# A streaming GLU kernel: stores moved to GpSimd's software queue, merged tile instructions, and fewer waits

## Chip, cores, metric

The kernel runs on one core of a Trainium2 chip. The metric is device time in microseconds (us) of one execution, median of several; all runs used below for a verdict are in the fast state (for one core: not over 1.5% above the fastest run of the same kernel). Profiles are of one execution each, and their span is some 2 us shorter than the device time.

## The reference

```python
# x: 8192 x 8192 float32, out: 8192 x 4096 float32
a, b = np.split(x, 2, axis=-1)
return a * (1 / (1 + np.exp(-b)))
```

So 268.44 MB come in, 134.22 MB go out, and each output element takes one sigmoid and one product.

## The kernel before

32 tiles; a tile is 128 partitions of two consecutive rows each, so one partition holds 64 KB of input and 32 KB of output, both contiguous in memory. There are two slots of each buffer. Loads are issued by SyncE, stores by ScalarE, both through hardware queues.

```python
R = 2
n_tiles = n_rows // (P * R)
x_t = x.rearrange("(n p r) m -> n p (r m)", p=P, r=R)
out_t = out.rearrange("(n p r) m -> n p (r m)", p=P, r=R)
pool = ctx.enter_context(tc.tile_pool(name="io", bufs=2))
for i in range(n_tiles):
    x_sb = pool.tile([P, R * n_cols], fp32)
    o_sb = pool.tile([P, R * half], fp32)
    load = nc.sync.dma_start(out=x_sb, in_=x_t[i])
    n = 4 if i == n_tiles - 1 else 1        # the last tile in 8 pieces
    w = half // n
    for r in range(R):
        for c in range(n):
            # ... a, b, cols: the piece's two inputs and its output columns
            nc.scalar.activation(out=b, in_=b, func=SIG)
            nc.vector.tensor_mul(out=o_sb[:, cols], in0=a, in1=b)
            if n > 1:
                nc.scalar.dma_start(out=out_t[i, :, cols], in_=o_sb[:, cols])
    if n == 1:
        nc.scalar.dma_start(out=out_t[i], in_=o_sb)
# ... the first load is moved ahead of the start barrier
```

## Time and profile before

| | before |
|---|---|
| device time, median of 6 runs | 936.02 us (935.64 to 936.99) |
| span of the profiled run | 933.9 us |
| DMA | 402.67 MB, 431 GB/s over the span |
| VectorE, ScalarE busy | 30%, 25% |
| load / store, issue to landing | 45.5 / 41.7 us |
| one tile every | 29.0 us |

Read it from the DMA rows down. The engines that compute are idle for 70 and 75% of the span, the DMA engines never; the two landing times are longer than the 29.0 us in which a tile passes, so in both queues a transfer stands behind its predecessor. The prediction shows and reads the lines.

### The profile page before, as it was taken

Reading aid. Unit: us, or ns where it says so; the run is one execution under the profiler, and the core shown is the slowest. Engines: PE = TensorE matmul, PEld = TensorE weight load, DVE = VectorE, ACT = ScalarE, POOL = GpSimd, SP = SyncE. Lnnn points to the kernel's source line nnn. Section 1 sums busy time; section 2 is a strip of 40 time slices with the busy share of each in tenths; the row PEclk is TensorE's granted clock in tenths of the full one; section 3 lists DMA queues with packets and bytes.
Section 4 is the critical chain, followed back from the end, with each engine's and each line's share of the span. In section 5 each row is a group of like instructions: output and inputs, shape, how many; then the busy total and the mean of one; then the engine's idle time right before and its main releaser. Section 6 shows DMA issues by size and latency. Waiting matters only on the chain.

```text
span 933.9 us, 410 instructions
## 1 busy us (share of the span) xinstructions
DVE 280.9 (30%) x70; ACT 230.0 (25%) x71; POOL 0.2 (0%) x4
## 2 busy tenths in 40 slices
DVE  0333321333213333133331333312333123331234
ACT  1313331133311333203332033320233202333023
POOL 0000000000000000000000000000000000000000
DMA  9999999999999999999999999999999999999998
GB/s 404 420 434 431 453 418 429 439 434 449 420 456 404 452 424 427 449 425 451 412 459 410 438 438 425 451 421 452 413 449 421 431 445 443 429 420 453 410 446 362
DMA packets 10226, 402.67 MB, mean 431 GB/s; under 512 B 1136, under 2 KB 1136, under 8 KB 2160
## 3 DMA queue, kind: packets, MB, share of 16 engines
q1 hardware_dynamic: 4608, 268.44, 66.5%
q10 hardware_dynamic: 5616, 134.22, 33.3%
q14 instruction: 2, 0.02, 0.0%
HBM read 268.44 MB, written 134.22 MB: 431 GB/s over the span
## 4 chain that ended last, share of the span: by engine, by line
DMA 78%; DVE 15%; ACT 6%; issue 0%; DVEq 0%; ACTq 0%
DMA x_sb<-in_x_dram 78%; DVE o_sb L39 15%; ACT x_sb L38 6%; DVEq L61 0%; ACTq L41 0%; ACTq L38 0%
## 5 line engine op out<-in xcount | busy, mean ns | idle before, releaser
L39 DVE TENSOR_TENSOR o_sb<-x_sb 128x4096 f32<-128x4096 f32 (+1 forms) x70 | 280.9, 4056 | 647.2 <-ACT x_sb L38 647.2
L38 ACT ACTIVATE x_sb<-x_sb 128x4096 f32<-128x4096 f32 (+1 forms) x70 | 228.7, 3315 | 695.9 <-DMA x_sb<-in_x_dram 691.8
L38 ACT ACT_TABLE_LOAD x1 | 1.3, 1283 | 0.8 <-PEq L85 0.8
L85 POOL MEMSET const-uint8-127<- 128x1 uint8 x1 | 0.1, 103 | 0.0
L85 POOL MEMSET const-bfloat16-1.0<- 128x1 bf16 x1 | 0.1, 102 | 0.0
L85 POOL MEMSET const-float32-0.0<- 128x1 f32 x1 | 0.1, 99 | 0.2 <-issue 0.2
L85 POOL MEMSET const-float32-1.0<- 128x1 f32 x1 | 0.1, 99 | 0.0
## 6 DMA issues: line engine op xcount, KB each, us to landing
out_dram<-o_sb ACTq DMA_DIRECT2D x31, 4096.0 KB, 41.7
out_dram<-o_sb ACTq DMA_DIRECT2D x8, 512.0 KB, 6.2
x_sb<-in_x_dram SPq DMA_DIRECT2D x32, 45.5
```

The lines of the kernel that those rows point to most:

```text
L38: nc.scalar.activation(out=b, in_=b, func=SIG)
L39: nc.vector.tensor_mul(out=o_sb[:, cols], in0=a, in1=b)
L85: nc = _bacc.Bacc("TRN2", target_bir_lowering=False, num_devices=1)
```

## The change

The intent: let GpSimd, which has nothing to do, issue the stores; compute each tile in one sigmoid and one product instead of two and two; and declare away every wait that follows from one that is kept, so that fewer instructions wait. In odd tiles the wait for the output slot moves from the product to the sigmoid ahead of it.

```diff
-            nc.scalar.activation(out=b, in_=b, func=SIG)
-            nc.vector.tensor_mul(out=o_sb[:, cols], in0=a, in1=b)
...
-    if n == 1:
-        nc.scalar.dma_start(out=out_t[i], in_=o_sb)
+    load = nc.sync.dma_start(out=xs[i % SLOTS], in_=x_t[i])
+    implied(load, *old["loads"], *old["sigs"])
...   # parts: tile 0 in two halves, tiles 1 to 30 whole, the last in eight pieces
+    for k, (r, c) in enumerate(parts):
+        b = rows[:, r, 1, c]
+        sig = nc.scalar.activation(out=b, in_=b, func=SIG)
+        mul = nc.vector.tensor_mul(out=packed[:, r, c], in0=rows[:, r, 0, c], in1=b)
+        implied(sig, *old["sigs"], *old["muls"], *old["loads"])
+        implied(mul, *old["muls"], *old["loads"], *now["loads"])
+        by_sigmoid = i % 2 == 1 and len(parts) == 1
+        implied(mul, *(s for s in old["stores"] if by_sigmoid or s not in freed))
+        if by_sigmoid:
+            for s in freed:
+                tc.add_manual_dep(sig.ins, s.ins.name, DEP, reason="frees the output slot")
...
+    now["stores"].append(nc.gpsimd.dma_start(out=out_t[i], in_=os[i % SLOTS]))
```

More of the change, by code (lines that the diff above doesn't have):

```diff
@@ L11, in _tiles @@
     P = nc.NUM_PARTITIONS
+    DEP = mybir.DependencyInfo(mybir.DependencyClass.Sync, mybir.DependencyReason.DATA)
     fp32 = mybir.dt.float32
@@ L17, in _tiles @@
     R = 2
+    SLOTS = 2
     n_tiles = n_rows // (P * R)
@@ L20, in _tiles @@
     out_t = out.rearrange("(n p r) m -> n p (r m)", p=P, r=R)
-    pool = ctx.enter_context(tc.tile_pool(name="io", bufs=2))
-    first = None
-    for i in range(n_tiles):
-        x_sb = pool.tile([P, R * n_cols], fp32)
-        o_sb = pool.tile([P, R * half], fp32)
-        load = nc.sync.dma_start(out=x_sb, in_=x_t[i])
-        first = first or load
-        n = 4 if i == n_tiles - 1 else 1
-        w = half // n
-        for r in range(R):
-            for c in range(n):
-                lo = r * n_cols + c * w
-                a = x_sb[:, lo : lo + w]
-                b = x_sb[:, lo + half : lo + half + w]
-                cols = slice(r * half + c * w, r * half + (c + 1) * w)
-                nc.scalar.activation(out=b, in_=b, func=SIG)
-                nc.vector.tensor_mul(out=o_sb[:, cols], in0=a, in1=b)
-                if n > 1:
-                    nc.scalar.dma_start(out=out_t[i, :, cols], in_=o_sb[:, cols])
-        if n == 1:
-            nc.scalar.dma_start(out=out_t[i], in_=o_sb)
@@ L44, in _tiles, with implied @@
-    return first
+    pool = ctx.enter_context(tc.tile_pool(name="io", bufs=1))
+    xs = [pool.tile([P, R * n_cols], fp32, name=f"x_sb{k}") for k in range(SLOTS)]
+    os = [pool.tile([P, R * half], fp32, name=f"o_sb{k}") for k in range(SLOTS)]
+    def implied(later, *earlier):
+        for e in earlier:
+            tc.declare_no_dep(later.ins, e.ins, reason="follows from the waits that are kept")
+    gone = [{k: [] for k in ("loads", "sigs", "muls", "stores")} for _ in range(SLOTS)]
+    last_stores = [[] for _ in range(SLOTS)]
@@ new lines, in _tiles @@
+    for i in range(n_tiles):
+        old = gone[i % SLOTS]
+        freed = last_stores[i % SLOTS]
+        now = {k: [] for k in old}
+        rows = xs[i % SLOTS].rearrange("p (r h m) -> p r h m", r=R, h=2)
+        packed = os[i % SLOTS].rearrange("p (r m) -> p r m", r=R)
+        load = nc.sync.dma_start(out=xs[i % SLOTS], in_=x_t[i])
+        implied(load, *old["loads"], *old["sigs"])
+        now["loads"].append(load)
+        if i == 0:
+            parts = [(slice(r, r + 1), slice(0, half)) for r in range(R)]
+        elif i < n_tiles - 1:
+            parts = [(slice(0, R), slice(0, half))]
+        else:
+            w = half // 4
+            parts = [
+                (slice(r, r + 1), slice(c * w, (c + 1) * w)) for r in range(R) for c in range(4)
+            ]
+        for k, (r, c) in enumerate(parts):
[9 more added lines that the diff above has]
+                    tc.add_manual_dep(sig.ins, s.ins.name, DEP, reason="frees the output slot")
+            now["sigs"].append(sig)
+            now["muls"].append(mul)
+            if i == n_tiles - 1:
+                cols = slice(r.start * half + c.start, r.start * half + c.stop)
+                store = nc.gpsimd.dma_start(out=out_t[i, :, cols], in_=os[i % SLOTS][:, cols])
+                now["stores"].append(store)
+        if i < n_tiles - 1:
+            now["stores"].append(nc.gpsimd.dma_start(out=out_t[i], in_=os[i % SLOTS]))
+        for s in now["stores"]:
+            implied(s, *old["loads"], *old["sigs"], *old["muls"], *now["loads"], *now["sigs"])
+        for k in old:
+            old[k] += now[k]
+        last_stores[i % SLOTS] = now["stores"]
```

## The prediction

> **What bounds the kernel now.** I read the share of the 16 DMA engines first, then the DMA queues, then stretches of the span, and only then the chain of work that ended last, because the chain alone misleads here. The page says that the DMA engines are the only thing that is full:
>
> ```profile
> DVE 280.9 (30%) x70; ACT 230.0 (25%) x71; POOL 0.2 (0%) x4
> ...
> DMA  9999999999999999999999999999999999999998
> ...
> q1 hardware_dynamic: 4608, 268.44, 66.5%
> q10 hardware_dynamic: 5616, 134.22, 33.3%
> ...
> HBM read 268.44 MB, written 134.22 MB: 431 GB/s over the span
> ```
>
> Queue q1 is the loads, q10 the stores. Their packets took 66.5% + 33.3% = 99.8% of what 16 engines have in 933.9 us, that is 932 us. So the time of the packets is the whole span. Cost per byte is the same in both directions: 0.665 x 933.9 / 268.44 = 2.31 us per MB for loads and 0.333 x 933.9 / 134.22 = 2.32 us per MB for stores. Next, stretches of the span: one tile in the middle, the loading of the last tile, and the end.
>
> ```profile
> 420.00:449.00 29.00, 8.76 (x2) 7.12 (x2) 0.00 (x0) 1.00 1.00 434
> ...
> 898.25:914.69 16.44, 0.00 (x0) 0.00 (x0) 0.00 (x0) 1.00 1.00 435
> ...
> 930.00:931.00 1.00, 0.00 (x0) 0.00 (x0) 0.00 (x0) 1.00 1.00 410
> 931.00:932.00 1.00, 0.00 (x0) 0.00 (x0) 0.00 (x0) 1.00 0.43 172
> 932.00:933.00 1.00, 0.00 (x0) 0.00 (x0) 0.00 (x0) 1.00 0.04 16
> ```
>
> The last two columns are the DMA share and GB/s. A tile is 8.39 MB in and 4.19 MB out, 12.58 MB, and the tiles are 29.0 us apart: 12.58 / 29.0 = 434 GB/s at a share of 1.00. The engines stay full until about 931.4; only the first 1 to 2 us (the first packets are booked between 1 and 2 us) and the last 2.5 us are without data. The loss that any scheduling change could recover is therefore some 4 us of 934, and most of it is the latency of the first and the last transfer.
>
> Now the chain:
>
> ```profile
> 172.24 45.44 DMA x_sb<-in_x_dram
> 217.76 3.62 ACT x_sb L38
> 221.41 8.77 DVE o_sb L39 x2
> 230.20 45.41 DMA x_sb<-in_x_dram
> ```
>
> It reads as load, sigmoid, two products, next load into the same slot, every 58.0 us for two tiles. The trap is to think that compute of 12.4 us is on this path. The load issued at 172.24 does not run 45 us: another tile's data landed at 188.91 (the sigmoids there start at that time), so for its first 16.7 us it stands in its queue behind the other load, and then it moves in 28.8 us. The chain thus has 16.7 us of slack that the profile paints as DMA. The stores have such a queue too: landing is 41.7 us after issue, with one issued every 29 us, so each stands some 12.6 us behind the one before.
>
> **What the Trainium skill says.** "DMA: Bandwidth & Descriptors", section "Where 436 GB/s comes from": the fabric caps the 16 engines at 435.2 GB/s. The trace agrees: 434 to 435 in full stretches. Same page, "Queues, rings and completion order": an engine goes round its queues packet by packet. The trace agrees: a load has one row of 64 KB in each of 128 partitions and a store one of 32 KB, so packets taken in turn split the bytes 2:1. That is also what the kernel needs, and both queues indeed stay backlogged. "SWDGE vs HWDGE vs iDMA", still the same page: the software path prefers packets of at most 4096 bytes; no run shows it yet. "SBUF — State Buffer", section "Who interferes with whom": GpSimd, which writes the descriptors of its stores, shares a port pair with VectorE, but a product of two SBUF inputs collides only with GpSimd reads. No run yet shows GpSimd stores.
>
> **The change part by part.** (1) One sigmoid and one product for both rows of a tile, in 30 of 32 tiles. From the groups by shape:
>
> ```profile
> L39 DVE TENSOR_TENSOR o_sb<-x_sb 128x4096 f32<-128x4096 f32 x62 | 271.6, 4422 | 626.6 <-ACT x_sb L38 626.6
> L38 ACT ACTIVATE x_sb<-x_sb 128x4096 f32<-128x4096 f32 x62 | 220.8, 3608 | 670.1 <-DMA x_sb<-in_x_dram 670.1
> L39 DVE TENSOR_TENSOR o_sb<-x_sb 128x1024 f32<-128x1024 f32 x8 | 9.4, 1221 | 20.6 <-ACT x_sb L38 20.6
> L38 ACT ACTIVATE x_sb<-x_sb 128x1024 f32<-128x1024 f32 x8 | 7.9, 1046 | 25.9 <-DMA x_sb<-in_x_dram 21.8 <-DVE o_sb L39 4.1
> ```
>
> Two sizes give a line: sigmoid (3608 - 1046) / 3072 = 0.834 ns per element and 192 ns fixed, so 8192 elements take 7.02 us; product 1.042 ns and 154 ns, so 8.69 us. Saved: 30 x 0.19 = 5.8 us of ScalarE and 30 x 0.15 = 4.6 us of VectorE, both three quarters idle: worth 0. Lost: the product no longer starts after half the sigmoid. From landing to the end of the product it was 12.4 us; it becomes 7.02 + 8.69 + two hops of 0.03 = 15.8 us. So the next load and the store are issued 3.3 us later. The load has 16.7 us of slack: 13.4 left. The store has about 12.6: 9 left. On the path to the end: 0. The first tile keeps its halves and the last its eight pieces.
>
> (2) Waits. Odd tiles wait for the old store before the sigmoid instead of before the product. A store is issued 12.47 us after its tile landed and is through 41.7 us later, at +54.2; the tile two later lands at +58.1. The sigmoid therefore finds it done with 3.9 us to spare. If it came later by some us, it would eat from the 13.4 us of the load. The trace before has 153 semaphore instructions that stand alone (17 to 21 ns each), in engines that wait anyway; dropping some of them is worth 0.
>
> (3) Stores by GpSimd. Software has to write the descriptors first, which no row here times; with 9 us of backlog in front, some microseconds of it are worth 0 for 31 stores. Bytes are the same, so the packet time stays at 932 us if the packets stay one row each. ScalarE no longer issues stores in the last tile: it sat 4.1 us there for products, so pieces come out about a microsecond earlier. But store 30 lands 24.8 us after 898.25, at 923.05, while the last load lands at 914.69; the eight pieces need 8 x 0.52 MB / 0.434 = 9.7 us behind it, to 932.7 with receipt, and the last landed at about 933.1. So the end is full of DMA too, and earlier pieces only queue. Worth 0 to -0.5. For the software path's completion and the drain of one more engine's queue I add an estimate of 0.5 to 1 us, without a row behind it.
>
> Sum: 936.13 + 0 + 0 - 0.3 + 0.8 = about 936.6.
>
> **The rivals.** A: the software queue cuts a row of 32 KB into small packets. The end of the trace prices it: with 4 KB rows a full engine moves 410 GB/s, not 434, so 134.22 MB would take 327 instead of 309 us, +18 us. Worse, in a turn by packets loads would get nearly everything, stores would fall behind, products wait for output slots, and the load queue run dry while one store plus 15.8 us of computing pass: 1 to 5 us for each pair of tiles, +16 to +80. For it: the packet size that the skill names for that path. Against: a contiguous row needs no cut, and the hardware path cuts none (q1's 4608 packets are 4096 rows and 32 x 16 completions). Result 954 to 1030; chance 6%.
>
> B: the opposite, several rows sent per turn. Stores finish early, loads still always have work, but the last load lands later and less is left for the stores behind it; the last pieces come at landing + 12 us instead of lying in a backlog. At most 3 us: 937 to 940. Chance 10%.
>
> C: the chain as painted is real, and 3.3 us more per tile and slot lengthens it: 16 x 3.3 = +53 us, 989. Against: a DMA share of 1.00 in every inner tile; a chain that set the pace would leave gaps. 1%.
>
> D: the new path is faster by something, for instance in fewer waits. Against: the packets alone need 932 us of the 933.9. To gain 2%, the rate would have to reach 442 GB/s, above anything in a long stretch. Under 1%.
>
> **Range and chances.** The floor is stiff: below 935 nothing can come but a shorter tail, so the low end is 935.0. Upward, B and a slower completion reach 940, and part of A lies beyond; high end 941. The 2% line is 954.9, which only A and C pass: slower 0.07, faster 0.01, same 0.92.
>
> **What would show it.** Right: DMA share 9 in every slice; a software queue of 134.22 MB at about 33.3% with a packet for each row; loads landing 29.0 us apart; load time to landing shrinking from 45.5 to about 42.2, as the slack is eaten; merged sigmoid 7.0 and product 8.7 us; idle of ScalarE still ended by loads, not by stores. Wrong: many more packets in the store queue or a higher share per MB (A); sigmoids or products ended by stores, with slices of DMA under 9 (A, C); landings of stores well under 40 us with a thin tail (B).

## The result, and the profile after

| | before | after |
|---|---|---|
| device time, median of 6 runs | 936.02 us | 936.49 us (936.21 to 937.22) |
| span of the profiled run | 933.9 us | 934.7 us |
| instructions in the profile | 410 | 286 |
| semaphore instructions that stand alone, in the loop | 153 | 77 |
| load / store, issue to landing | 45.5 / 41.7 us | 42.1 / 38.2 us |

The ratio is 1.0005, 95% interval 0.9992 to 1.0018: the same. (A ratio here is the mean time of one kernel's runs over that of the other's in the same rounds, so not quite the ratio of the medians.) The page of the changed kernel, the same parts as in the prediction:

```profile
DVE 278.7 (30%) x40; ACT 227.0 (24%) x41; POOL 21.1 (2%) x43
...
DMA  9999999999999999999999999999999999999998
...
q1 hardware_dynamic: 4608, 268.44, 66.5%
q0 software_dynamic: 5616, 134.22, 33.3%
```

The stores are now in a software queue, q0. Its count of packets, its bytes and its share are those of the hardware queue before, to the digit: 5616, 134.22 MB, 33.3%. The DMA engines do the same work in the same time, and they are still full. The changed kernel's chain in order of time, and its merged instructions by shape:

```profile
117.57 42.24 DMA x_sb<-in_x_dram
159.90 7.04 ACT x_sb L66
166.96 8.70 DVE o_sb L67
175.68 42.02 DMA x_sb<-in_x_dram
```

```profile
L67 DVE TENSOR_TENSOR o_sb<-x_sb 128x8192 f32<-128x8192 f32 x30 | 260.7, 8692 | 605.7 <-ACT x_sb L66 605.7
L66 ACT ACTIVATE x_sb<-x_sb 128x8192 f32<-128x8192 f32 x30 | 210.9, 7029 | 652.2 <-DMA x_sb<-in_x_dram 652.2
```

Computing takes 3.3 us longer in each link of the chain (7.04 + 8.70 instead of 3.62 + 8.77), and the painted load is 3.4 us shorter (42.0 to 42.2 instead of 45.4), so a link still takes 58.1 us (58.0 before). The later issue was paid out of queueing. The idle time of ScalarE is still ended by loads, never by a store: the wait that moved to the sigmoid costs nothing here.

Only the end differs. The instructions that close the program, for the kernel before (columns: count, duration in ns as minimum/median/maximum, first and last start in us):

```profile
L61 POOLq DRAIN  x3: 34/41/70, 0.7 to 933.7; - x3
L61 SPq DRAIN  x3: 7/7/7, 933.2 to 933.5; - x3
```

and for the changed kernel:

```profile
L104 POOLq DRAIN  x3: 45/101/9608, 924.3 to 934.4; - x3
L104 SPq DRAIN  x3: 7/7/7, 932.7 to 934.2; - x3
```

SyncE reaches its first drain when all stores have landed: at 933.2 before, at 932.7 after. From there to the end of the span it was 0.7 us; now it is 2.0 us, because GpSimd has a drain of 9.6 us, begun after its last issue at 924.3, that holds the closing barrier until about 933.9. So -0.5 us for landing, +1.3 us for closing: +0.8 us of span, of which +0.5 us shows in the medians.

### The profile page after: what moved, and what is told of

The parts are those of the page before. It is cut to its first block, busy times and chain, and to the rows that moved or that the text cites. A ratio compares the mean times of both kernels' runs of the same rounds, so it can differ in the third digit from the quotient of the medians.

```text
span 934.7 us, 286 instructions
## 1 busy us (share of the span) xinstructions
DVE 278.7 (30%) x40; ACT 227.0 (24%) x41; POOL 21.1 (2%) x43
## 3 DMA queue, kind: packets, MB, share of 16 engines
q0 software_dynamic: 5616, 134.22, 33.3%
HBM read 268.44 MB, written 134.22 MB: 431 GB/s over the span
## 4 chain that ended last, share of the span: by engine, by line
DMA 72%; DVE 14%; ACT 11%; issue 1%; POOL 0%; POOLq 0%; ACTq 0%
DMA x_sb<-in_x_dram 72%; DVE o_sb L67 14%; ACT x_sb L66 11%; POOL out_dram L79 0%; POOLq L104 0%; ACTq L66 0%; POOLq L79 0%
## 5 line engine op out<-in xcount | busy, mean ns | idle before, releaser
L67 DVE TENSOR_TENSOR o_sb<-x_sb 128x8192 f32<-128x8192 f32 (+2 forms) x40 | 278.7, 6983 | 645.4 <-ACT x_sb L66 645.4
L66 ACT ACTIVATE x_sb<-x_sb 128x8192 f32<-128x8192 f32 (+2 forms) x40 | 225.7, 5661 | 693.7 <-DMA x_sb<-in_x_dram 693.7
L82 POOL DMA_DIRECT2D out_dram<-o_sb x31 | 16.6, 536 | 884.5 <-DVE o_sb L67 884.5
L79 POOL DMA_DIRECT2D out_dram<-o_sb x8 | 4.2, 531 | 19.1 <-DVE o_sb L67 19.1
## 6 DMA issues: line engine op xcount, KB each, us to landing
out_dram<-o_sb POOLq DMA_DIRECT2D x31, 4096.0 KB, 38.2
x_sb<-in_x_dram SPq DMA_DIRECT2D x32, 42.1
```

The lines of the kernel that those rows point to most:

```text
L66: sig = nc.scalar.activation(out=b, in_=b, func=SIG)
L67: mul = nc.vector.tensor_mul(out=packed[:, r, c], in0=rows[:, r, 0, c], in1=b)
L79: store = nc.gpsimd.dma_start(out=out_t[i, :, cols], in_=os[i % SLOTS][:, cols])
L82: now["stores"].append(nc.gpsimd.dma_start(out=out_t[i], in_=os[i % SLOTS]))
```

## The experiments

Twelve runs, each three rounds beside the kernel before. The first two take the change apart; e3, e4, e10 and e11 measure the slack; e5, e6, e9 and e12 ask what the packets and the place of a wait would do; e7 and e8 look at the end. A run can count as the same (under 2%) and still differ clear of noise, when the interval of its ratio leaves out 1.

### Stores alone: e1_stores_only

```diff
-nc.scalar.dma_start(...)        # in the kernel before, both stores
+nc.gpsimd.dma_start(...)
```

> The kernel before with nothing changed but the issuer of the stores (GpSimd instead of ScalarE). My theory (the DMA engines' packet time is the bound, and the software queue adds only something at the very end): 936.0 to 937.0 us, a span of about 934.7 us as in the changed kernel, one software queue of 134.22 MB at 33.3%, 5616 packets, share of DMA 1.00 in the middle; GpSimd's last drain ends over 1 us after the last landing. Rival (the software queue costs something in every tile, which the merged instructions give back): a tile period above 29.05 us and more than 940 us. Rival (the software queue costs nothing, the end comes from the merge): 933.9 us of span.

Measured: 937.56 us (937.28 to 938.12), ratio 1.0017 (1.0002 to 1.0032), span 935.4 us. The software queue again has 5616 packets and 33.3%; SyncE's first drain is at 933.4, the end 2.0 us later, with a GpSimd drain of 9.5 us. The closing cost is the same as in the changed kernel; the median lies 0.6 us above the range that I wrote. Nothing is lost per tile: loads land 45.5 us after issue, as before.

### Merged instructions and fewer waits alone: e2_merge_only

```diff
-nc.gpsimd.dma_start(...)        # in the changed kernel, both stores
+nc.scalar.dma_start(...)
```

> The changed kernel with its stores issued by ScalarE again, so merged instructions and fewer waits alone. The instruction order shows a side effect: in every fourth tile the store stands behind the next tile's sigmoid in ScalarE's queue, so it is issued some 20 us later. My theory: loads fill the DMA engines meanwhile and the load has 13 us of slack, so 935.5 to 936.5 us and a span of 933.5 to 934.2 us, without GpSimd's long drain at the end. Rival (merging costs time, and the software stores hide it): more than 940 us, with slices of DMA under 9.

Measured: 942.73 us (939.46 to 945.34), ratio 1.0069 (1.0045 to 1.0094). My expectation failed by 6 us; the rival's time fits, but not its gaps in the DMA row. Who waited for whom in this run:

```profile
ACT x_sb L66 <- DMA out_dram<-o_sb: 362.8, 12, 34.5
ACT x_sb L66 <- DMA x_sb<-in_x_dram: 334.7, 20, 22.1
DVE o_sb L67 <- DMA out_dram<-o_sb: 168.0, 12, 18.0
```

Sigmoids and products now wait for stores, which they do in neither kernel. In every fourth tile the store stands behind the next tile's sigmoid in ScalarE's queue, goes out late, and through the output slots the lateness reaches the loads. Slices of DMA all stay at 9, yet the load queue's share is 66.7% of 941.6 us, or 628 us for the bytes that took 621 us before: the loss is in longer load packets. So the parts of the change are not independent: with stores in ScalarE's in-order queue the merged form with its moved waits costs 0.7%, and moving the stores to GpSimd takes that away. Whether the merge or the wait that moved to the sigmoid is needed for the loss, no run separates: none has the merged form with stores by ScalarE and the wait before the product.

### More compute: e3_two_products, e4_three_products

```diff
 mul = nc.vector.tensor_mul(out=packed[:, r, c], in0=rows[:, r, 0, c], in1=b)
+if len(parts) == 1:
+    for _ in range(1):               # e4: range(2)
+        mul = nc.vector.tensor_mul(out=packed[:, r, c], in0=rows[:, r, 0, c], in1=b)
```

> The changed kernel, each merged product done twice (the same result): 8.7 us more between a load's landing and the next load into that slot, from 15.9 to 24.6 us. My theory: the load has about 13 us of slack behind the other load, so 936 to 937 us, DMA share 9 throughout, and the loads' time from issue to landing falls from 42.1 to about 33.4 us. Rival (the painted chain is real): one slot's cycle of two tiles is 8.7 us longer, 15 times 8.7 = 130 us, so about 1067 us.

Measured: 977.45 us (974.09 to 981.74), ratio 1.0445 (1.0414 to 1.0475). My expectation failed, and so did the rival's 1067. I had looked at the load's 13 us of slack and forgotten the store's 9 us, which the prediction itself gives: 8.7 us more uses it up but for some 0.5 us. In 14 tiles a sigmoid waited for a store. But the page shows something else that I had not thought of:

```profile
DMA  9999999999999999999999999999999999999997
...
q1 hardware_dynamic: 4608, 268.44, 67.3%
q0 software_dynamic: 5616, 134.22, 31.8%
```

The DMA engines are as busy as ever, and the loads' packets take 67.3% of 980.0 us, 660 us instead of 621. 39 of the 46 us more of span are in slower load packets, not in gaps. A full DMA row proves that the engines have work, not that the work goes at full rate; the cost per MB (2.46 instead of 2.31 us) is the thing to compare.

> The changed kernel, each merged product done three times: 33.3 us between landing and the next load, more than the 29.0 us in which the other slot's load lands. My theory: now the slack is used up; the load queue runs dry for about 4 us in each tile, the loads' time to landing is that of a load that starts at once (28 to 31 us), one slot's cycle of two tiles is 33.3 + 28 to 31 us, so 31 to 32 us per tile: 990 to 1030 us, and the DMA share falls below 0.95. Rival (compute never matters while VectorE is under 100%): 936 us. Rival (painted chain): two times 130, about 1197 us.

Measured: two runs at 1056 us, two at 1087 us; the profile has 1054.4 us. The direction is as expected and the size is above my range. VectorE is busy 76%, loads land 31.2 us after issue, and the DMA share in the middle is 0.90 to 0.91. In 14 tiles a sigmoid waited for a store, 397 us in all, which no run takes out here. The packet records show a second loss beside the emptied queue: a load gives each of the 16 engines eight rows, so it goes in eight rounds of packets, and the first two rounds took 3.0 and 3.1 us on average, the others 2.42 to 2.45. So the load packets take 662 us instead of 621, 40 of the 120 us more of span. The two slow rounds seem to go with different queues. The first follows an empty load queue, like the first round of the whole program, which takes 3.1 us in the kernels before and after. The second mostly ends just as the packets of a store begin after an empty store queue. Before and after have one such round too, where no load is late: the last of the second load, 3.6 us, ends at 42 us, and the first store's packets begin at 41.3 and 41.5 us.

### Half of that: e11_half_product_more

```diff
+if len(parts) == 1:
+    now["muls"].append(mul)
+    mul = nc.vector.tensor_mul(out=packed[:, 1, c], in0=rows[:, 1, 0, c], in1=rows[:, 1, 1, c])
```

> The changed kernel with only half of each merged product done a second time: 4.4 us more instead of 8.7. The change itself spent 3.3 of the store's 12.6 and the load's 16.7 us. Theory (slack is what counts, the store's 9 us being the smaller): 4.4 us fit, 936 to 937.5 us, loads landing about 37.7 us after issue, stores about 33.8. Rival (every delay costs in proportion, as 8.7 us cost 41 us): about 957 us.

Measured: 936.59 us (936.42 to 937.33), ratio 1.0006 (0.9991 to 1.0021); loads land after 37.7 us, stores after 33.7 us, both as written. 133 us more of VectorE's time cost nothing at all. So the slack is real, between 4.4 and 8.7 us of it are left in the changed kernel, and beyond it time is lost out of proportion. The issues of this run (the last number is the median time to landing):

```profile
out_dram<-o_sb POOLq DMA_DIRECT2D x31, 4096.0 KB, 33.7
...
x_sb<-in_x_dram SPq DMA_DIRECT2D x32, 37.7
```

### Is it the wait before the sigmoid? e10_two_products_late_wait

```diff
-by_sigmoid = i % 2 == 1 and len(parts) == 1     # in e3
+by_sigmoid = False
```

> The run with two products per tile again (977 us), all tiles waiting for the old store before the product. Theory W: the store, issued 8.7 us later, used up the 9 us of its backlog, and the odd sigmoid that waited for it (14 times, 336 us) made loads late; with the wait 7 us later the load is in time and the kernel is back at 936 to 942 us. Theory L (a load issued only 4 us ahead of its queue's end is what slows it, whoever is to blame): 965 to 980 us.

Measured: 979.4 us (969.08 to 980.68), ratio 1.047 (1.0453 to 1.0488). Theory W fell: now no sigmoid and no product waits for a store, and it is as slow. Two tiles early and two stretches in the middle of this run (the last two columns are DMA share and GB/s):

```profile
72.00:101.00 29.00, 17.39 (x2) 6.97 (x2) 0.53 (x1) 1.00 1.00 434
101.00:130.00 29.00, 17.39 (x2) 7.04 (x2) 0.53 (x1) 1.00 1.00 434
...
400.00:430.00 30.00, 17.38 (x2) 6.81 (x2) 0.53 (x1) 1.00 1.00 419
430.00:460.00 30.00, 17.39 (x2) 6.55 (x2) 0.53 (x1) 1.00 1.01 415
```

It starts at the full 434 GB/s with each load issued some 4.3 us ahead of its turn, and then slides to 415 at the same share. In the packet records the first two rounds of a load take 2.8 and 2.7 us on average, nearly as long as where the queue is quite empty (e4), and after the slide the starts of one round are spread over 3 to 4 us instead of 0.6 to 1.0 in the kernels before and after.

Theory L's range fits, but that a load issued too shortly before its queue runs out is what costs is not shown. The same run speaks against it as a rule: its loads were issued some 4.3 us ahead from load 3 on, and the first rounds of loads 3 to 11 (counted from 0) still took 2.42 us. A rival is untested: the stores were issued 8.7 us later too, which leaves the store queue only some 0.5 us (38.2 - 8.7 - 29.0), and e4's second slow round goes with the store queue, not with the load queue. No run makes only the loads or only the stores late. So 8.7 us of delay in both queues is too much; which queue it is, why such packets are slower, and what starts the slide stay open.

### Small packets in the software queue: e5_small_software, e6_half_rows

```diff
-now["stores"].append(nc.gpsimd.dma_start(out=out_t[i], in_=os[i % SLOTS]))
+o4 = os[i % SLOTS].rearrange("p (j t w) -> p j t w", t=2, w=1024)    # e6: w=4096
+d4 = out_t[i].rearrange("p (j t w) -> p j t w", t=2, w=1024)         # e6: w=4096
+for t in range(2):
+    now["stores"].append(nc.gpsimd.dma_start(out=d4[:, :, t, :], in_=o4[:, :, t, :]))
```

> The changed kernel with each full store cut into pieces of 4 KB (two stores of a tile, each taking every other 4 KB of a row), still in the software queue: the forecast's rival A made by hand. From the last tile's 4 KB rows (410 against 434 GB/s) the packets alone cost about 15 to 18 us more. Theory T (queues take turns packet by packet): a store gets 4 KB for each 64 KB of a load, so stores wait nearly until the loads are done, sigmoids or products wait for output slots, the load queue runs dry, and there are slices with DMA under 9: 960 to 1030 us. Theory B (queues share by bytes, whatever the packets): 950 to 955 us, landings of stores near 38 us and loads 29 us apart as now. Theory N (small packets cost nothing in this queue): 936.5 us.

Measured: 982.72 us (981.78 to 984.16), ratio 1.0498 (1.0482 to 1.0514). Theory T's range, though not its slices with DMA under 9: all but the last stay at 9. While a load and a store are both under way, 10 us of this run (queue: packets, MB, share of 16 engines):

```profile
q1 hardware_dynamic: 64, 4.19, 96.7%
q0 software_dynamic: 64, 0.26, 6.4%
```

64 packets against 64: turns, whatever the packets hold. One term of the price was near: the 4 KB packets took 33.3% of 982.2 us, 327 us for the stores, as the prediction worked out from the last tile. The rest is in load packets again (646 us) and in some idle time. Products waited 532 us and sigmoids 450 us for stores.

> The changed kernel with each full store cut in two stores of 16 KB rows in the software queue. Packets: 134 MB in twice as many, some 2 us more. Theory T (turns by packet): a store gets 16 KB for each 64 KB while a load runs, 20% instead of 33%, so two loads pass quickly and stores catch up while the load queue is empty; little or no idle time of the DMA engines, 937 to 950 us, but products or sigmoids wait for stores, which they did not. Theory B (by bytes): 937 to 939 us and all waits as in the changed kernel.

Measured: 1079.96 us (1076.21 to 1087.01), ratio 1.1522 (1.1487 to 1.1557). Turns again: from 430 to 440 us it was 64 load packets and 63 store packets, 3.15 against 0.79 MB, 80:20. But the time is 130 us above my range and 97 us worse than with packets a quarter as large. Stretches of one pair of tiles in this run:

```profile
418.27:455.00 36.73, 0.00 (x0) 0.00 (x0) 1.06 (x2) 1.00 1.01 426
...
463.49:470.00 6.51, 0.00 (x0) 6.51 (x1) 0.00 (x0) 1.00 1.02 438
470.00:479.50 9.50, 8.95 (x2) 7.44 (x2) 0.00 (x0) 1.00 0.02 7
```

(Columns: stretch and length in us, busy time and instructions of VectorE, ScalarE and GpSimd, TensorE's clock, DMA share, GB/s.) The odd tile's load, issued at 409.4, is in 29.2 us later, at 438.6; the store that frees its output slot lands only at 463.5. Only then does the sigmoid start, then the product, and the next load waits for both: from 470 the DMA engines have nothing to do for 9.5 us.

### The same with the wait before the product: e9_half_rows_late_wait

```diff
-by_sigmoid = i % 2 == 1 and len(parts) == 1     # in e6
+by_sigmoid = False
```

> The run with stores of 16 KB rows again, with one difference: all tiles wait for the old store before the product, none before the sigmoid. In that run (1080 us) the odd sigmoid waited 56 us for stores and held up the even tile's sigmoid behind it, and no DMA moved for 7 us of each pair. Theory W (the wait before the sigmoid is what makes late stores so dear): sigmoids are done when the stores land, the pair needs two products of 8.7 us instead of sigmoid and products, most of the idle time goes: 945 to 985 us. Theory T alone (turns by packet, the place of the wait doesn't matter): 1060 to 1090 us again.

Measured: 983.46 us (977.21 to 984.32), ratio 1.0491 (1.0458 to 1.0523). Theory W: 97 us of the 144 go. My wording of it was partly off: it is not so much that the odd sigmoid holds up the even one (whose load landed at 463.1, hardly sooner) as that the odd sigmoid's own 7.0 us come between the landing of the store and the next load. For 15 pairs that is 105 us, near the 97. With the wait at the product the sigmoid runs while the store is under way. In the changed kernel stores are not late, so this trap is set and never sprung.

### Loads cut as well: e12_half_rows_both

```diff
-load = nc.sync.dma_start(out=xs[i % SLOTS], in_=x_t[i])          # on top of e6
+for r in range(R):
+    cols = slice(r * n_cols, (r + 1) * n_cols)
+    load = nc.sync.dma_start(out=xs[i % SLOTS][:, cols], in_=x_t[i, :, cols])
```

> The run with stores of 16 KB rows again (1080 us), but the loads also cut in two, of 32 KB rows, so that a store's packet is again half of a load's. Theory T (queues take turns packet by packet): bytes split 2:1 again, stores keep up, 937 to 942 us, packets of loads and stores cost 2 to 4 us more in all. Rival (small packets or two stores per tile are what hurts on the software queue): 1000 us or more.

Measured: 940.84 us (940.73 to 940.89), ratio 1.005 (1.0035 to 1.0065). With a store packet half a load packet again, 140 us vanish, though there are still more packets and transfers, and the wait still stands before the odd sigmoid. The page of this run:

```profile
q1 hardware_dynamic: 9216, 268.44, 66.3%
q0 software_dynamic: 10080, 134.22, 33.4%
```

So it was not small packets nor the software queue that hurt in e6, but the ratio of the rows: turns by packet give each queue a share in proportion to its packet. (The loads now also come as two transfers for each tile; no run has that alone.)

### The end: e7_last_by_scalar, e8_last_by_gpsimd

```diff
-store = nc.gpsimd.dma_start(...)      # changed kernel, the last tile's eight stores
+store = nc.scalar.dma_start(...)      # e8: the opposite, in the kernel before
```

> The changed kernel with only the last tile's eight stores issued by ScalarE. My theory (the 0.8 us more of span are GpSimd's drain at the end, which lasts more than a microsecond past the last landing): GpSimd's last drain ends early, and the span is 933.2 to 934.0 us, against 934.7. Rival (the 0.8 us lie elsewhere, e.g. in later stores all along): 934.7 us.

Measured: 935.47 us (935.31 to 935.62), span 933.8 us. The closing instructions of this run:

```profile
L104 POOLq DRAIN  x3: 45/93/22823, 901.4 to 933.1; - x3
L104 SPq DRAIN  x3: 7/7/7, 932.6 to 932.9; - x3
```

GpSimd's long drain, begun after its last issue at 901.4, is over at about 924.2, well before SyncE's at 932.6, and 0.9 us of the span are gone although all stores land as in the changed kernel. From SyncE's first drain to the end it is 1.2 us instead of 2.0, so the drain is where most of the closing cost was; some 0.4 us over the 0.7 of the kernel before remain. This version has the shortest time of all, but its ratio to the kernel before is 0.9992 (0.9977 to 1.0007): not clear of it.

> The kernel before with only the last tile's eight stores issued by GpSimd. My theory: the last data land 0.5 to 1 us sooner, since ScalarE no longer waits for products in the last tile, but GpSimd's drain adds over 1 us: a span of 934.5 to 935.0 us against 933.9. Rival (the drain costs nothing by itself): 933.0 to 933.9 us.

Measured: 936.27 us, ratio 1.0001 (0.9986 to 1.0016), span 934.6 us. The number is in my range, and not for my reason: SyncE's first drain came at 933.8, so the stores landed later, not sooner, and GpSimd's drain (7.0 us from 926.7) ended at about the same moment, not over 1 us later. With eight stores in the software queue the closing takes 0.8 us, with 39 it takes 2.0, and with the 70 of e6, e9 and e12 it takes 3.3; but e5, with 70 stores of 4 KB rows, takes 1.4, so the count alone does not set it. What the drain does in that time no run shows.

## Why the prediction was right

Predicted 936.6 us in 935.0 to 941.0; measured 936.49. The reason held: the packets fill the span, and the change alters neither their number nor their bytes. That the number fits to 0.1 us is luck: the interval of the ratio alone is 2.4 us wide.

- **The bound.** Right: 932 us of packets before, and the same packets, bytes and shares after. That computing is not the limit was also tested: 133 us more of VectorE in e11 changed nothing.
- **Merged instructions.** Right to 0.01 us: sigmoid 7.02 us predicted, 7.03 measured; product 8.69, 8.69. Issue 3.3 us later; landing of loads 42.2 predicted, 42.1 measured.
- **The slack.** Right: 9 us was given for the store and 13.4 for the load; the store's 38.2 us less the 29.0 us of a tile leave 9.2. The experiments narrow it: 4.4 us more of computing fit, 8.7 do not.
- **The software queue.** Right in effect: one packet for each row. Its issue took GpSimd 0.53 us for each store, off the path; it took the same 0.53 us in the last tile, beside running products, and those took 1218 ns against 1221 before, so nothing here collides.
- **The end.** The total was right, its parts too small: -0.3 predicted and -0.5 measured for landing, +0.8 predicted and +1.3 measured for closing. The estimate without a row behind it is the one that was most off. The sign of the landing term was luck as well: its reason, that ScalarE no longer issues the last stores, does not fit the other runs. In the kernel before with the last stores by GpSimd, SyncE's first drain came at 933.4 (e1) and 933.8 (e8), later than 933.2; in the changed kernel with them by ScalarE (e7) it came at 932.6, as early as 932.7. These are single profiles, and the spans of the kernel before differ by 1.5 us between runs. One sum was off too: the 9.7 us for the eight pieces use 434 GB/s where the prediction's own line has 410 for such rows, which gives 10.2 us.
- **Rival C** (the painted chain sets the pace, 989 us) is refuted by the changed kernel: compute in a link grew by 3.3 us and the link did not. **Rival A** was priced about right for 4 KB (954 to 1030; 982.7 measured by hand-made packets), but its reason for the stalls was incomplete: a good part of the loss sits in load packets that get slower, at a full DMA row. **Rivals B and D** did not occur.

What the forecast missed is that the merge with its moved waits is only free because the stores left ScalarE (e2), and that the moved wait is a hazard as soon as stores are late (e6 against e9).

## What to carry to other kernels

When the packets' time fills the span, ask of each part of a change only whether it alters packets or eats slack, and take the smallest slack of all the buffers, not the one of the loads alone. Watch the cost per MB of each queue besides the DMA row: here the row stayed at 9 while a kernel lost 4.5%. Queues that share the DMA engines take turns by packet, so keep the row sizes of loads and stores in the ratio of their bytes, and keep loads and stores issued well ahead of the end of their queues (8.7 us for loads with 4.7 for stores were enough here, 4.3 with 0.5 were not).

## What the Trainium skill lacked or had wrong

- "DMA: Bandwidth & Descriptors", "SWDGE vs HWDGE vs iDMA", speaks of packets of at most 4096 bytes as preferred in the software queue. Here that queue sent 32 KB rows as single packets, as the profile counts them: 5616 packets, which are 31 x 128 rows, 8 x 128 pieces and 39 x 16 completions, the same count as in the hardware queue.
- Same page, "Queues, rings and completion order", gives turns of whole packets of typically 9 to 17 descriptors. Here a turn is one row: in the changed kernel 16 rows of a load, then 16 of a store follow each other in the records, and it is 64 packets against 64 with rows of 64 KB and 4 KB (e5), 64 against 63 with 64 and 16 KB (e6). That the share of a queue therefore follows its row size, worth 1080 against 941 us (e6, e12), is not said there.
- I found it on no page: packets of a load are slow when its queue had been empty, 3.0 instead of 2.42 us for 64 KB (e4, first round), and in the round in which a store queue that had been empty starts again, 3.1 us (e4, second round) and 3.6 us (before and after, second load); this is busy time in the DMA row.
- I found it on no page: GpSimd's drain at the end of the program holds the closing barrier, 2.0 us from SyncE's first drain to the end with 39 stores in the software queue, 3.3 with 70 (e6, e9, e12; 1.4 in e5), 0.7 with none.
